# A two-layer decoder step on eight cores: channel-major residual, five blocks of 416 tokens, and one planned instruction order

## The chip, the cores and the metric

The kernel runs on all 8 cores of one Trainium2 chip. Each core takes one prompt sequence of 2048 tokens and four of the 32 sample sequences with 8 new tokens each, so 2080 tokens, and all the weights. The cores do not talk to each other. The metric is the device time of the slowest core, in microseconds (us).

Executions come in two states. In the fast state the eight cores lie within about 2% of each other. In the slow state the cores of one die (sometimes of both) show a lower granted TensorE clock and the time is some per cent longer.

## The reference, cut to what matters

```python
D_MODEL = 1024; SEQ = 2048; DEPTH = 2; D_FF = 4096; HEAD_DIM = 64
DIL_PAIRS = ((128, 1), (512, 4), (2048, 16))        # (window, dilation), 2 heads each
IN_COLS = 2560                                      # u 256 | q,k,v 3 x 384 | gates 3 x 384

def trunk_layer(x, pos, is_prompt, ...):
    h = rmsnorm(x, norm1_g)
    proj = h @ w_in                                 # split into u, q, k, v, gb, gc, gh
    y_pool = pool_mix(pool_hist, u, pos, ...)       # causal means over 2/4/8/16 rows
    q = partial_rope(rmsnorm(q, q_norm_g), pos)     # rotary on 16 of 64 dims
    k = partial_rope(rmsnorm(k, k_norm_g), pos)
    for g, (window, dil) in enumerate(DIL_PAIRS):   # keys at distance 0, dil, ..., window
        o, lse = dilated_attention(q[g], k[g], v[g], window, dil)
    y_attn = sum over g of softmax(lse)[g] * o[g]   # = sum of numerators / sum of denominators
    z = gc * gh; y_conv = gb * conv3(z)
    x = x + concat(y_pool, y_attn, y_conv) @ w_out  # 768 -> 1024
    hf = rmsnorm(x, norm2_g) @ w_up                 # 1024 -> 4096
    x = x + square(relu(hf)) @ w_down               # 4096 -> 1024
    # ... also returned: the shifted K/V caches, pool and conv states
```

## The kernel before

The kernel before works stage by stage. The residual X lies token-major (128 tokens by 1024 channels, 17 tiles, the last one 32 tokens). Every norm scales a tile and then turns it with TensorE transposes into HT, the channel-major operand of the next matmuls:

```python
for t in range(NTILE):                                  # norm_and_transpose, 17 tiles, 4 times a run
    S.op("dve", ... scalar_tensor_tensor(out=hb, in0=X[:, t, :], scalar=RSTD[:, t:t+1], in1=GBC, mult, mult))
    for c in range(8):
        S.op("pe", ... transpose(out=pst[:, c, 0:R], in_=hb[0:R, c*128:(c+1)*128], identity=IDB))
    S.op("act", ... copy(out=HT[:, :, 128*t:128*t+R], in_=pst[:, :, 0:R]))
```

Attention masks by adding a mask with a second matmul, and needs separate matmuls for the denominators:

```python
for (ki, kb) in kbs:                                    # att_unit, one of 16 per group
    matmul(pS[:, ki*256:+256], lhsT=K tile, rhs=Q of 2 heads, start=True, stop=False)
    matmul(pS[:, ki*256:+256], lhsT=IDB, rhs=MASKP, start=False, stop=True)       # mask
# ... exp ...
    matmul(pO[hs, 0:128], lhsT=VAUG[:, tk, h, 0:64], rhs=P, ...)                  # values
    matmul(pO[:, 128:256], lhsT=HSEL[:, h, :], rhs=P, ...)                        # denominators
# ... the three groups are summed into ACC by ACT or DVE, and divided after all of them
```

The MLP takes four blocks of 512 tokens and a last one of 32, for which the down projection still runs 512 columns wide:

```python
for fb in range(4):                 # 1024 hidden channels at a time
    up(0); copy_caches(l, fb)       # cache copies wait in hardware for the buffer ("at", 0)
    for b in range(5):              # b < 4: 512 tokens; b == 4: 32 tokens
        if b + 1 < 5: up(b + 1)     # 8 x 8 matmuls of blk_len(b) columns
        down(b)                     # per 128-token tile 2 x 8 matmuls of 512 columns, lhsT=at[:, fc, tile]
# ... the order of all instructions is the order in which this program text emits them
```

## Time and profile before

| | the kernel before |
|---|---|
| median of the first 3 runs | 1889.73 us (1887.67 to 1890.29) |
| TensorE (PE) busy | 1588.9 us, 84% of the span |
| VectorE (DVE) / ScalarE (ACT) busy | 47% / 32% |
| chain of work that ended last | PE 74%, DVE 8%, DMA 8% |

The page's busy times, then its strips of 40 slices (each digit the busy tenths of a slice; PEclk the granted TensorE clock in tenths; DMA the mean share of 16 engines), then the chain by engine:

```profile
PE 1588.9 (84%) x9076; PEld 806.7 (43%) x9076; DVE 895.9 (47%) x1593; ACT 599.9 (32%) x1255; POOL 199.0 (11%) x262
...
PE   0549768765899999999998985876579999999998
...
PEclk9979878957799999999997997895779999999999
DMA  9530001285440632603843000129544061260222
...
PE 74%; DVE 8%; DMA 8%; issue 5%; ACT 4%; POOL 1%; DVEq 0%; ACTq 0%; POOLq 0%; SPq 0%
```

The two runs of nines are the two MLPs. An average hides the rest, so here is the table of busy time by stretch. Each line has the stretch and its length in us, then per engine busy us and instructions, then the granted clock, the DMA share and GB/s:

```profile
core 6: us, PE busy (x) PEld busy (x) DVE busy (x) ACT busy (x) POOL busy (x), PEclk, DMA share, GB/s
0.00:88.00 88.00, 17.75 (x142) 13.56 (x143) 22.69 (x28) 38.16 (x58) 9.05 (x15) 1.00 0.77 165
395.00:446.00 51.00, 21.19 (x180) 12.38 (x178) 27.86 (x37) 12.10 (x29) 0.74 (x1) 0.50 0.66 161
494.00:520.00 26.00, 16.66 (x137) 12.83 (x138) 22.28 (x20) 17.42 (x20) 2.22 (x3) 0.56 0.80 122
520.00:990.00 470.00, 468.17 (x2368) 214.10 (x2366) 187.51 (x295) 101.30 (x194) 18.63 (x25) 0.99 0.40 72
1100.00:1342.00 242.00, 161.63 (x1255) 104.49 (x1255) 138.49 (x351) 125.22 (x321) 17.96 (x40) 0.77 0.31 79
1415.00:1887.00 472.00, 466.29 (x2368) 213.57 (x2366) 188.29 (x296) 83.43 (x162) 6.66 (x9) 1.00 0.30 63
```

So the MLPs (520 to 990 and 1415 to 1887) are TensorE at full clock with nothing to squeeze but the work itself. In the other 945 us TensorE is partly starved: in the end of attention (395 to 446) TensorE works 21 of 51 us at half clock, and in the norm stage (494 to 520) it works at a clock of 0.56. The trace shows the clock fall from 1.00 to 0.50 after a long pause and after short ones. At 496.9 us it falls in a pause of 4.7 us before the first transposes. At 377.4 us it falls too, and there no pause in the 15 us before lasted over 1.5 us; it stays at half through pauses of up to 2.9 us until 429 us. So a stream with many short pauses lost the clock here. The 1.00 of the first line isn't a measurement: the trace has no clock record before 90.7 us, and eight transposes took 1.01 us there, as they did from 498 us on at half clock.

In the chain inside an MLP, in order of time (start, duration, what), 64 matmuls of 512 columns (L1331, the down projection) take 13.81 us, 215.8 ns each. In the QKV stage, at full clock, 16 matmuls of 384 columns (L1014) take 2.61 us, 163.1 ns each. On the straight line through the two, 416 columns come to 176 ns, an estimate from these two numbers:

```profile
605.02 13.81 PE psum L1331 x64
```

```profile
338.74 2.61 PE psum L1014 x16
```

Two lines of the list of DMA issues (source, queue, count, KB each, median us to landing): the copies of the old caches (kv_s<-c, here the third of them that have 504 KB) and the pieces of w_out.

```profile
kv_s<-c SPq DMA_DIRECT2D x8, 504.0 KB, 9.4
...
big<-w_out POOLq DMA_DIRECT2D x6, 512.0 KB, 5.5
```

### The profile page before, as it was taken

To read this page: it belongs to the slowest core of one execution; us is meant where nothing else is said; L and a number is where in the kernel's file an instruction comes from. 1 tells how busy PE (TensorE), PEld (TensorE's weight loads), DVE (VectorE), ACT (ScalarE), POOL (GpSimd) and SP (SyncE) were. 2 spreads that over 40 slices of the span, in tenths; PEclk is the share of its full clock that TensorE was granted. 3 is DMA by queue.
4 is the path that set the end of the run, shared out by engine and by line. 5 is a ranking of instruction groups with operands and counts; after the bars stand their busy time and mean duration, and the time that the engine had idled before them with its cause. 6 is when DMAs were issued, how large, how long until landed. Compare 5 with 4: busy or idle time off the path is not lost.

```text
span 1887.7 us, 28589 instructions; the slowest of 8 cores (1875.0 to 1887.7 us)
## 1 busy us (share of the span) xinstructions
PE 1588.9 (84%) x9076; PEld 806.7 (43%) x9076; DVE 895.9 (47%) x1593; ACT 599.9 (32%) x1255; POOL 199.0 (11%) x262
## 2 busy tenths in 40 slices
PE   0549768765899999999998985876579999999998
PEld 0314445532444444444444443553244444444444
DVE  0427654736734444344337665473663443444433
ACT  3402356632521111212334235663252111121210
POOL 0147100000000000000003720000000000000000
PEclk9979878957799999999997997895779999999999
DMA  9530001285440632603843000129544061260222
GB/s 243 75 46 1 15 24 39 91 185 175 67 82 1 100 63 35 113 1 50 176 98 63 1 15 22 42 85 187 179 62 87 1 112 37 42 107 1 47 101 93
DMA packets 76348, 139.91 MB, mean 74 GB/s; under 512 B 28360, under 2 KB 41858, under 8 KB 75818
## 3 DMA queue, kind: packets, MB, share of 16 engines
q0 software_dynamic: 42144, 47.26, 17.5%
q1 hardware_dynamic: 34058, 90.83, 17.4%
q8 instruction: 77, 1.26, 0.3%
q14 instruction: 69, 0.57, 0.1%
HBM read 162.45 MB, written 44.75 MB: 110 GB/s over the span
## 4 chain that ended last, share of the span: by engine, by line
PE 74%; DVE 8%; DMA 8%; issue 5%; ACT 4%; POOL 1%; DVEq 0%; ACTq 0%; POOLq 0%; SPq 0%
PE psum L1331 25%; PE psum L1314 24%; PE psum L777 7%; PE psum L1014 7%; PE psum L1295 5%; DMA big<-w_in 5%; DVE big L714 2%; DMA big<-c 2%; DVE big L1270 1%; PE psum L720 1%; DVE big L1055 1%; ACT big L1023 1%; PE psum L1143 1%; DVE big L1157 1%; PE psum L1137 1%
## 5 line engine op out<-in xcount | busy, mean ns | idle before, releaser
L1331 PE MATMUL psum<-big 128*128 128x512 bf16 (+1 forms) x2176 | 477.4, 380 | 0.5 <-DVE big L1319 0.3
L1314 PE MATMUL psum<-big 128*128 128x512 bf16 (+1 forms) x2560 | 466.4, 340 | 1.5 <-DVE big L1319 1.3
L1318 ACT ACTIVATE big<-psum 128x512 f32<-128x512 f32 (+1 forms) x320 | 165.3, 517 | 690.0 <-PE psum L1314 681.6
L1319 DVE TENSOR_TENSOR big<-psum,big 128x512 bf16<-128x512 f32 (+1 forms) x320 | 189.2, 591 | 301.9 <-ACT big L1318 294.0
L1314 PEld LDWEIGHTS psum<-big 128*128 128x128 bf16 x2560 | 216.2, 98 | 249.6 <-issue 9.1
L1331 PEld LDWEIGHTS psum<-big 128*128 128x128 bf16 (+1 forms) x2176 | 211.9, 98 | 258.6 <-issue 6.3
L1333 DVE TENSOR_TENSOR big<-psum,big 128x512 f32<-128x512 f32 (+1 forms) x272 | 187.9, 691 | 261.4 <-PE psum L1331 261.2
L777 PE MATMUL psum<-big 128*128 128x512 bf16 (+1 forms) x880 | 166.0, 346 | 0.8 <-DVE big L897 0.4
L1014 PE MATMUL psum<-big 128*128 128x384 bf16 (+1 forms) x816 | 152.6, 347 | 15.2 <-ACT big L1023 6.7
L720 PE MATMUL psum<-big 128*128 128x128 bf16 (+1 forms) x544 | 66.0, 299 | 98.8 <-DVE big L714 98.0
L1014 PEld LDWEIGHTS psum<-big 128*128 128x128 bf16 (+1 forms) x816 | 96.0, 122 | 63.4 <-issue 31.8
L777 PEld LDWEIGHTS psum<-big 128*128 128x128 bf16 x880 | 75.2, 99 | 89.0 <-issue 9.4
L720 PEld LDWEIGHTS psum<-big 128*128 128x128 bf16 (+1 forms) x544 | 50.5, 136 | 115.4 <-issue 115.4
L1295 PE MATMUL psum<-big 128*128 128x512 bf16 (+1 forms) x408 | 93.7, 394 | 0.0
L714 DVE SCALAR_TENSOR_TENSOR big<-big 128x1024 bf16<-128x1024 f32 (+1 forms) x68 | 85.3, 1282 | 15.1 <-DMA big<-norm_g 9.4
L705 ACT ACTIVATE big<-big 128x1024 bf16<-128x1024 f32 (+1 forms) x51 | 53.9, 1057 | 76.2 <-DVE big L1297 58.3
L722 ACT COPY big<-psum 128x1024 bf16<-128x1024 bf16 (+1 forms) x68 | 65.9, 975 | 37.7 <-PE psum L720 37.7
L1157 DVE TENSOR_TENSOR big<-psum,big 128x256 f32<-128x256 f32 x64 | 39.2, 613 | 76.9 <-PE psum L1143 76.8
L667 POOL DMA_DIRECT2D big<-w_up x16 | 12.1, 758 | 586.6 <-PE psum L1314 329.3
L1297 DVE TENSOR_TENSOR big<-psum,big 128x512 f32<-128x512 f32 (+1 forms) x68 | 47.0, 691 | 48.9 <-PE psum L1295 48.9
L1295 PEld LDWEIGHTS psum<-big 128*128 128x128 bf16 (+1 forms) x408 | 40.8, 101 | 52.1 <-issue 7.7
L830 DVE SCALAR_TENSOR_TENSOR big<-big 64x512 bf16<-64x512 f32 (+1 forms) x40 | 35.7, 892 | 57.5 <-POOL big L817 50.5
(117 smaller groups left out, 1269.9 us busy)
## 6 DMA issues: line engine op xcount, KB each, us to landing
big<-xp SPq DMA_DIRECT2D x32, 512.0 KB, 12.2
big<-w_up POOLq DMA_DIRECT2D x16, 1024.0 KB, 11.0
big<-w_down POOLq DMA_DIRECT2D x16, 1024.0 KB, 15.6
kv_s<-c SPq DMA_DIRECT2D x8, 2040.0 KB, 20.1
big<-c SPq DMA_DIRECT2D x24, 512.0 KB, 5.2
xpark<-big SPq DMA_DIRECT2D x16, 512.0 KB, 3.7
big<-xpark SPq DMA_DIRECT2D x16, 512.0 KB, 9.7
yp<-big SPq DMA_DIRECT2D x16, 512.0 KB, 2.7
```

What stands on the lines that cost most here:

```text
L714: S.op("dve", lambda e, t=t, R=R, hb=hb: e.scalar_tensor_tensor(out=hb[0:R, :], in0=X[0:R, t, :], scalar=RSTD[0:R, t:t + 1], in1=GBC[0:R, ...
L720: S.op("pe", lambda e, c=c, R=R, hb=hb, pst=pst: e.transpose(out=pst[:, c, 0:R], in_=hb[0:R, c * 128:(c + 1) * 128], identity=IDB[0:R, 0:R ...
L722: S.op("act", lambda e, t=t, R=R, pst=pst: e.copy(out=HT[:, :, 128 * t:128 * t + R], in_=pst[:, :, 0:R]), reads=[("ps", pi)], writes=[("ht ...
L777: S.op("pe", lambda e, d=d, pi=pi, L=L: e.matmul(bank(pi)[:, 0:L], lhsT=WA[:, d, col0:col0 + 128], rhs=HT[:, d, blk_cols(b)], start=(d == ...
L1014: S.op("pe", lambda e, d=d, j=j, csel=csel: e.matmul(pqv[0:R, j, 0:384], lhsT=HT[:, d, csel], rhs=WQ[g][:, d, :], start=(d == 0), stop=(d ...
L1157: S.op("dve", lambda e: e.tensor_tensor(out=ACC[:, :, qsel], in0=pov, in1=ACC[:, :, qsel], op=ALU.add), reads=[("ps", po), "acc"], writes= ...
L1295: S.op("pe", lambda e, c=c, pi=pi, R=R, t=t, hf=hf: e.matmul(bank(pi)[0:R, :], lhsT=MIXT[:, c, tile_cols(t)], rhs=WO[:, c, 512 * hf:512 * ...
L1314: S.op("pe", lambda e, d=d, fc=fc, pi=pi, L=L: e.matmul(bank(pi)[:, 0:L], lhsT=WU[i][:, d, 128 * fc:128 * fc + 128], rhs=HT[:, d, blk_cols ...
L1318: S.op("act", lambda e, pi=pi, L=L, ri=ri: e.activation(out=RL[ri][:, 0:L], in_=bank(pi)[:, 0:L], func=AF.Relu), reads=[("ps", pi)], write ...
L1319: S.op("dve", lambda e, pi=pi, L=L, ri=ri, at=at, fc=fc: e.tensor_tensor(out=at[:, fc, 0:L], in0=bank(pi)[:, 0:L], in1=RL[ri][:, 0:L], op= ...
L1331: S.op("pe", lambda e, fc=fc, pi=pi, R=R, lo=lo, hf=hf, at=at: e.matmul(bank(pi)[0:R, :], lhsT=at[:, fc, lo:lo + R], rhs=WD[i][:, fc, 512 ...
L1333: S.op("dve", lambda e, pi=pi, R=R, t=t, hf=hf: e.tensor_tensor(out=X[0:R, t, 512 * hf:512 * hf + 512], in0=bank(pi)[0:R, :], in1=X[0:R, t ...
```

## The change

The intent: remove the transposes and the token tail, thin out the attention, and let a planner interleave stages that used to stand one after the other.

- **Channel-major residual.** X is kept as 8 x 128 channels by tokens, from input to output (the host lays the arrays out that way). The output and down projections now have the weights stationary and tokens as columns, so their results are channel-major too. The norm's sum over channels becomes a matmul with a matrix of ones in float32r; the 17 x 8 transposes of each norm go.
- **Five blocks of 416 tokens**: 5 x 416 = 2080, no tail.
- **Attention** on pairs of PSUM banks: the mask becomes a 0/1 multiplication on VectorE after the exponential; the value matmul's weights are [V | ones] (128 columns), so numerators and denominators of all three groups accumulate in two banks that stay held; one division per head and token block of 512.
- **Order from a plan.** Each stage is a generator with a priority. A simulation on the host with an assumed cost for each operation picks, at every moment, the ready operation of the lowest priority number for each engine. What comes out is a fixed order per engine; the semaphores between engines are real, so a wrong guess costs waiting. What the plan alone places, nothing holds.

The core of it as a diff, cut heavily (`...` marks cuts):

```diff
+LAT = {"pe": 0.25, "act": 0.12, "dve": 0.12, "pool": 0.15}
+class Planner:
+    def start(self, eng):                     # engine free, an operation ready
+        _, _, op, p = heapq.heappop(self.ready[eng])        # lowest priority number first
+        emit()                                # the instruction takes its place in the order
+        if len(op) > 3:                       # a DMA: 260 GB/s, one after the other, 2 us more
+            self.dma_free = max(self.dma_free, self.now) + nbytes / 260e3
+            done = max(self.dma_free, self.now) + 2.0
...
-        S.op("dve", ... scalar_tensor_tensor(out=hb, in0=X[0:R, t, :], scalar=RSTD, in1=GBC ...))
-        for c in range(8): S.op("pe", ... transpose(...))
-        S.op("act", ... copy(out=HT[:, :, 128 * t:128 * t + R], in_=pst))
+        for c in range(8):                    # norm(l, which, b): one block of 416 tokens
+            act(BL, activation(out=SQR[i], in_=X[:, b, c, :], func=Square))
+            pe(matmul(bank(bi)[:, 0:BL], lhsT=ONESR, rhs=SQR[i], start=(c == 0), stop=(c == 7)))   # float32r
+        act(Ln, scale=1/D, bias=EPS); act(Exp, scale=-0.5)
+        for c in range(8):
+            dve(scalar_tensor_tensor(out=HT[:, c, block b], in0=X[:, b, c, :], scalar=gain, in1=RST, mult, mult))
...
-    matmul(pS, lhsT=IDB, rhs=MASKP, start=False, stop=True)
-    matmul(pO[hs, 0:128], lhsT=VAUG[:, tk, h, 0:64], rhs=P)
-    matmul(pO[:, 128:256], lhsT=HSEL[:, h, :], rhs=P)
+    dve(tensor_tensor(out=P, in0=P, in1=MASKP, op=mult))
+    matmul(bank(6 + h)[...], lhsT=VREG[:, 8 * g + sl, 64 * h:64 * h + 128], rhs=P, start=first)   # [V | ones]
+    # att(): after all groups of a block of 512 tokens
+    RATT = exp(-ln(denominators))
+    dve(tensor_tensor(out=MIXT[hs, 2, c0:c0+512].rearrange("p (i r) -> p r i", r=16),
+                      in0=bank(6 + h)[hs] as (r i), in1=RATT[hs] as (r i), op=mult))
...
-    down: matmul(bank(pi)[0:R, :], lhsT=at[:, fc, lo:lo + R], rhs=WD[i][:, fc, 512 * hf:512 * hf + 512])
+    down: matmul(bank(bi)[:, 0:416], lhsT=WD[i][:, f, 128 * oc:128 * oc + 128], rhs=AT[a][:, f, :])
...
+    # mixer(l): priorities; lower comes first
+    K.spawn(norm(l, 0, b, ...), base + 2 + b)                 # base = 1000 * l
+    K.spawn(qkv(l, None, g, 0), base + 95)                    # the sample tokens' q, k, v
+    K.spawn(qkv(l, blk, g, pr), base + 100 + 50 * blk + 2 * g + pr)
+    K.spawn(seq(all of pool and conv done, load_wo(l, 2)), base + 400)     # the third piece of w_out
+    K.spawn(reload(l, b, done[b]), base + 300)                # x comes back for the residual
+    # mlp(l): the waits of the weight loads
+    if fb == 0: wu, wd = qk_done, att_done
...
-    copy_caches: S.dma(..., reads=[("at", 0)])                # waits in hardware
+    copy_caches: wait(ev("um", l, fb, 1, 0)) then ld(...)     # waits in the plan only
```

## The prediction

> **What bounds it now.** TensorE work, plus stages that starve it. The table of busy time by stretch (slowest core) splits 1887.7 us into two MLP stages of 470 and 472 us, where PE is busy 99% at a granted clock of 0.99 to 1.00, and about 945 us of everything else: 520 us before the first MLP, 425 us between the MLPs. In those 945 us PE is busy about 655 us, part of it slow: clock 0.52 to 0.60 in the norm-and-transpose stages (26, 27, 25 us), 0.50 in the ends of attention (50 us each, PE busy 21 to 23 us), and little before 88 us, where the chain is the serial w_in loads. Chain view: PE 74%.
>
> **MLP.** 64 matmuls of 512 columns take 13.81 us in the chain: 215.8 ns each. [...] Blocks of 416 should take 175.8 ns [...]. 5120 of them are 900 us, against 942 us: the change removes the tail (128 down matmuls of 512 columns for 32 tokens, and 512 small up matmuls). Gain about 40 us, all on the critical path.
>
> **Mixer, per layer, PE (estimates from the trace's rates).** Projections 440 x 175.8 ns = 77 us; QKV 408 x 163 ns = 66 (unchanged); output projection 240 x 175.8 = 42; attention about 35 to 40 (before 79: S, mask, value and denominator matmuls 158 us over two layers; mask matmuls go, value|ones merges two groups); sum-of-squares matmuls 80, 15 to 25 us (replacing 35 us of cold transposes); transposes, sample and pool 22. Sum about 265 us. DVE about 225 to 240 us (a 512-column op 0.69 us, scaled), ACT 185, POOL 80: PE stays the limit, DVE close behind. In before the attention stretch (1100 to 1342 us) kept PE busy for only 160 of 242 us, as stages were separate. The plan interleaves them; I expect 80 to 85% PE density: 310 to 330 us per mixer instead of 425.
>
> **Edges.** Start: x (8.5 MB) and weights at the 237 GB/s seen in the first 40 us; the WQ pieces still wait for each other (5.1 us each alone). QKV comes first, so PE works from about 35 us and the projections from about 110 us; I charge 50 us. Layer change: norms of blocks 0 to 3 run under the last MLP blocks; 10 to 15 us left of 27. Tail 8 us.
>
> **Sum.** 50 + 315 + 450 + 12 + 315 + 450 + 8 = 1600 us; I say 1595. Range 1530 to 1670 (8 in 10). Faster by over 2%: 0.95; within 2%: 0.03; slower: 0.02.
>
> **What would show it.** MLP: two stretches of about 450 us, PE 99%, 176 ns a matmul, clock 1.0. Mixers: PE busy 80 to 85%, clock above 0.9, no stretch at 0.5. PE busy in total about 1430 us. Output projection running into the MLP without a gap. ACT and DVE each below 75% in the mixers.
>
> **What would make it wrong.** [...] (b) The order is fixed from assumed costs; where a DVE, POOL or DMA step is later than planned, PE waits in order and falls to half clock: 30 to 60 us a mixer. (c) DVE with POOL beside it slows (a 512-column op with three operands took 0.87 to 1.05 us against 0.69), making DVE the limit. (d) Start loads slower than charged. (e) Better than thought: density of 90% gives 1540.

## The result, and the profile after

| | before | after |
|---|---|---|
| fast runs | 1887.67 to 1890.29 us (4 runs) | 1700.05, 1700.66, 1706.17 us |
| slow runs | none of the four | 1933.25, 1925.86, 1816.41 us |
| PE busy, slowest core | 1588.9 us (84%) | 1458.2 us (86%) |
| DVE / ACT / POOL busy | 47% / 32% / 11% | 52% / 28% / 15% |

The ratio of the fast runs is 0.901, with a 95% interval of 0.899 to 0.904. Ratios here are the mean time of one kernel's fast runs over that of the other's of the same rounds, so not quite the ratio of the medians quoted. The kernel became 10% faster, but its 1700 us lie 105 us above the predicted 1595 and above the range.

```profile
PE 1458.2 (86%) x8668; PEld 811.5 (48%) x8668; DVE 874.8 (52%) x1637; ACT 482.4 (28%) x1065; POOL 247.3 (15%) x342
...
PE   4466679629999999999997677876999999999998
...
PEclk9777999969999999999997889998999999999999
DMA  8662310599923206015154341007999320500022
...
PE 68%; DVE 11%; DMA 8%; issue 6%; POOL 4%; ACT 3%; DVEq 0%; ACTq 0%; SPq 0%; POOLq 0%
```

The nines of the MLPs are shorter, and the wide valleys at half clock are gone but for one slice just before the first MLP (the 2 among the PE digits, clock 6, DMA 9). Below it is the stretch from 349 to 383:

```profile
core 5: us, PE busy (x) PEld busy (x) DVE busy (x) ACT busy (x) POOL busy (x), PEclk, DMA share, GB/s
0.00:135.00 135.00, 64.61 (x247) 32.56 (x247) 50.99 (x122) 45.99 (x118) 39.62 (x63) 0.81 0.75 137
135.00:349.00 214.00, 161.97 (x1243) 95.18 (x1244) 149.05 (x295) 86.87 (x204) 74.99 (x98) 0.93 0.26 58
349.00:383.00 34.00, 2.49 (x10) 0.74 (x8) 5.17 (x3) 1.50 (x3) 1.46 (x2) 0.57 1.02 212
383.00:431.00 48.00, 47.70 (x255) 25.87 (x256) 29.36 (x52) 13.86 (x26) 0.00 (x0) 0.95 1.03 169
431.00:885.00 454.00, 454.00 (x2581) 252.53 (x2580) 202.48 (x348) 95.13 (x187) 22.27 (x28) 1.00 0.33 60
886.00:925.00 39.00, 30.42 (x101) 14.80 (x101) 21.24 (x34) 24.84 (x51) 10.43 (x20) 0.74 0.56 110
925.00:1182.00 257.00, 192.39 (x1362) 109.77 (x1360) 179.49 (x384) 104.23 (x266) 89.16 (x120) 0.89 0.28 53
1182.00:1238.00 56.00, 49.29 (x293) 27.02 (x293) 34.29 (x55) 15.56 (x29) 0.00 (x0) 0.90 1.02 226
1238.00:1692.00 454.00, 454.00 (x2581) 252.48 (x2579) 201.86 (x347) 94.33 (x184) 8.90 (x12) 1.00 0.31 63
```

(The 0.81 of the first line is too high, for the first 50 us have no clock record and count as 1.00: eight QKV matmuls took 2.74 us at 47.6 us, as they did at 61.4 us at half clock, 2.72 us; at 77 us, at full clock, sixteen took 2.97 us.)

Read it as two copies of the same work. From 0 to 431 us TensorE is busy for 277 us, from 886 to 1238 for 272 us (sums of the lines). The work is nearly the same; the waiting differs. In layer 0, TensorE is idle for 70 us up to 135, 52 us from 135 to 349 and 32 us from 349 to 383: 154 us in all. In layer 1 it is idle for 9, 65 and 7 us: 80 us. The first layer loses 74 us more, at its start and at its end.

From the time lines, the savings against the kernel before are: the stretch before the first MLP 520 to 431, the first MLP 470 to 454, between the MLPs 425 to 353, and the second MLP with the tail 472 to 460. That is 89 + 16 + 72 + 12 = 189 us.

In the chain, 128 matmuls of the MLP (L1318, the up projection) take 22.51 us, 175.8 ns each. At the MLP's start something stands between every 8 of them:

```profile
660.57 22.51 PE psum L1318 x128
```

```profile
431.61 1.42 PE psum L1318 x8
433.22 1.42 PE psum L1318 x8
```

Groups of 1.42 us start 1.61 us apart. In the 0.19 us between them stands one float32r matmul of 416 columns (a sum of squares of a later block), which the timeline shows there. So a float32r matmul costs about as much as a bf16 one (175.8 ns). Its weight load took 190 ns there on average (bf16: 98 ns), overlapped.

The chain of the start (start, duration, what), then the one step at the end of the first mixer:

```profile
4.89 11.98 DMA big<-w_in
...
17.41 21.32 DMA big<-w_in
...
68.41 5.44 DMA big<-w_in
...
73.98 2.72 PE psum L971 x8
```

```profile
349.44 33.72 DMA big<-w_out
```

What TensorE waited for (line, releaser, total us, times, longest), and the landings:

```profile
PE psum L799 <- ACT sqr L796: 38.7, 34, 9.7
PE psum L1302 <- DMA big<-w_out: 25.5, 1, 25.5
PE psum L971 <- DMA big<-w_in: 19.9, 2, 10.7
...
PE psum L1152 <- DVE big L1216: 8.8, 4, 3.6
...
PE psum L1302 <- DVE big L1216: 6.4, 1, 6.4
```

```profile
kv_s<-c SPq DMA_DIRECT2D x8, 504.0 KB, 56.9
...
big<-w_out POOLq DMA_DIRECT2D x6, 512.0 KB, 10.2
```

L971 is the QKV matmul, L1302 the output projection, L1216 the last division of attention, L1152 the value matmul, and L799 and L796 the sums of squares and the squares. The cache copies of 504 KB now take 56.9 us to land instead of 9.4, and all 24 copies are issued from 356.5 us on (for layer 0) and 1187.8 us on (for layer 1): before the MLP, not in it. Of the six w_out pieces the worst, the last one of layer 0, lands after 33.7 us. The last one of layer 1 lands after 10.1 us: there is no such stall before the second MLP.

### The profile page after: what moved, and what is told of

It reads as the page before. It is cut to its first block, busy times and chain, and to the rows that moved or that the text cites. A ratio compares the mean times of both kernels' runs of the same rounds, so it can differ in the third digit from the quotient of the medians.

```text
span 1697.8 us, 27200 instructions; the slowest of 8 cores (1680.6 to 1697.8 us)
## 1 busy us (share of the span) xinstructions
PE 1458.2 (86%) x8668; PEld 811.5 (48%) x8668; DVE 874.8 (52%) x1637; ACT 482.4 (28%) x1065; POOL 247.3 (15%) x342
## 4 chain that ended last, share of the span: by engine, by line
PE 68%; DVE 11%; DMA 8%; issue 6%; POOL 4%; ACT 3%; DVEq 0%; ACTq 0%; SPq 0%; POOLq 0%
PE psum L1318 27%; PE psum L1334 27%; PE psum L1302 5%; DMA big<-w_in 4%; PE psum L841 4%; PE psum L971 3%; DVE big L1019 2%; DMA big<-w_out 2%; POOL big L1011 2%; PE psum L799 2%; DVE big L1216 1%; DMA big<-spool 1%; DVE big L1005 1%; DMA big<-vspill 1%; DVE big L995 1%
## 5 line engine op out<-in xcount | busy, mean ns | idle before, releaser
L1318 PE MATMUL psum<-big 128*128 128x416 bf16 x2560 | 463.5, 339 | 0.0
L1334 PE MATMUL psum<-big 128*128 128x416 bf16 x2560 | 460.7, 339 | 0.0
L1323 ACT ACTIVATE big<-psum 128x416 f32<-128x416 f32 x320 | 165.4, 517 | 667.8 <-PE psum L1318 435.6
L1334 PEld LDWEIGHTS psum<-big 128*128 128x128 bf16 x2560 | 249.5, 98 | 199.9 <-issue 2.1
L1318 PEld LDWEIGHTS psum<-big 128*128 128x128 bf16 x2560 | 248.2, 98 | 200.1 <-issue 4.8
L1324 DVE TENSOR_TENSOR big<-psum,big 128x416 bf16<-128x416 f32 x320 | 188.2, 591 | 296.2 <-ACT big L1323 286.2
L1337 DVE TENSOR_TENSOR big<-psum,big 128x416 f32<-128x416 f32 x320 | 188.5, 591 | 204.4 <-PE psum L1334 203.9
L971 PE MATMUL psum<-big 128*128 128x384 bf16 (+1 forms) x816 | 167.8, 368 | 37.8 <-DMA big<-w_in 19.9
L841 PE MATMUL psum<-big 128*128 128x416 bf16 x880 | 182.3, 360 | 12.8 <-DVE big L1005 3.5
L971 PEld LDWEIGHTS psum<-big 128*128 128x128 bf16 (+1 forms) x816 | 85.8, 108 | 108.3 <-issue 70.7
L1302 PE MATMUL psum<-big 128*128 128x416 bf16 x480 | 97.0, 353 | 38.2 <-DMA big<-w_out 25.5
L841 PEld LDWEIGHTS psum<-big 128*128 128x128 bf16 x880 | 87.5, 103 | 84.5 <-issue 31.6
L796 ACT ACTIVATE sqr<-big 128x416 fp32r<-128x416 f32 x160 | 84.7, 544 | 144.5 <-PE psum L799 86.7
L818 DVE SCALAR_TENSOR_TENSOR big<-big 128x416 bf16<-128x416 f32 x160 | 95.2, 668 | 53.7 <-ACT big L817 52.7
L799 PE MATMUL psum<-sqr,onesr 128*128 128x416 f32 x160 | 84.4, 556 | 39.1 <-ACT sqr L796 38.7
L1011 POOL TENSOR_TENSOR big<-big 128x512 f32<-128x512 f32 (+1 forms) x54 | 67.8, 1257 | 141.2 <-DVE big L1005 121.5
L1302 PEld LDWEIGHTS psum<-big 128*128 128x128 bf16 x480 | 44.7, 100 | 80.6 <-issue 51.9
L1304 DVE TENSOR_TENSOR big<-psum,big 128x416 f32<-128x416 f32 x80 | 45.2, 590 | 63.6 <-PE psum L1302 60.6
L799 PEld LDWEIGHTS psum<-sqr,onesr 128*128 128x128 f32 x160 | 36.1, 226 | 67.5 <-issue 60.7
```

Source lines behind the costliest of these rows:

```text
L799: return pe([(BL, lambda e: e.matmul(bank(bi)[:, 0:BL], lhsT=ONESR[:, :], rhs=SQR[:, i * BL:(i + 1) * BL], start=(c == 0), stop=(c == 7)), ...
L818: yield ops(*[dve(BL, lambda e, c=c: e.scalar_tensor_tensor(out=HT[:, c, BL * b:BL * b + BL], in0=X[:, b, c, :], scalar=NG[:, l, which, c: ...
L841: yield ops(pe([(BL, lambda e, d=d: e.matmul(bank(bi)[:, 0:BL], lhsT=WA[:, d, col0:col0 + 128], rhs=HT[:, d, BL * b:BL * b + BL], start=(d ...
L971: yield ops(pe([(384, lambda e, d=d, j=j, jj=jj: e.matmul(pq[0:R, jj, 0:384], lhsT=lhs(d, j), rhs=WQ[g][:, d, :], start=(d == 0), stop=(d ...
L1011: yield ops(pool(256 * J, lambda e: e.tensor_tensor(out=qf[0:R, 0:J, 0:256], in0=qf[0:R, 0:J, 0:256], in1=GQK[0:R].unsqueeze(1).to_broadca ...
L1302: yield ops(pe([(BL, lambda e, c=c: e.matmul(bank(bi)[:, 0:BL], lhsT=WO[c // 2][:, c % 2, 128 * oc:128 * oc + 128], rhs=MIXT[:, c, BL * b: ...
```

## The experiments

All are variations of the changed kernel, each run on the same chip. "Ratio" is against the kernel before, from fast runs; the changed kernel itself stands at 0.901. Times are means of fast runs. All outputs agreed with the reference but for one experiment. Every edit is planned anew. In the traces of div_order and copy_pinned the instructions of every engine still stand in the order of the changed kernel; in the others the order can move as well, so a control (plan_shift) comes with them.

The time of the slowest core jitters: in some fast runs one or two cores run an MLP at a clock of 0.97 or 0.98 and end 10 to 20 us late. The mean over the fast runs of the median core is steadier, so the overview gives both (us). The starts of the MLPs are those of the slowest core of the profiled run.

| | slowest core | median core | first MLP starts | second MLP starts |
|---|---|---|---|---|
| the changed kernel | 1702 | 1690 | 431 | 1238 |
| norm_early | 1710 | 1695 | 428 | 1241 |
| div_order | 1687 | 1676 | 425 | 1227 |
| wo_first | 1701 | 1693 | 419 | 1238 |
| smp_late | 1679 | 1666 | 401 | 1218 |
| copy_pinned | 1691 | 1682 | 423 | 1227 |
| tail_order | 1678 | 1670 | 409 | 1213 |
| w_burst | 1701 | 1694 | 401 | 1239 |
| plan_shift | 1703 | 1689 | 417 | 1229 |
| three_fixes | 1652 | 1643 | 388 | 1187 |
| four_fixes | 1652 | 1638 | 392 | 1185 |
| burst_fixes | 1666 | 1658 | 412 | 1210 |
| rope_one | 1633 | 1624 | 385 | 1175 |
| start_order | 1674 | 1665 | 404 | 1213 |
| wq_burst3 | 1676 | 1667 | 407 | 1216 |
| slow_w20 | 1650 | 1643 | 391 | 1185 |
| slow_w15 | 1648 | 1642 | 384 | 1186 |

### 1. norm_early: the second layer's norms before the last MLP blocks

The prediction wanted the norms of layer 1 to run under the last MLP blocks; their priority (1002 and up) puts them behind all of the MLP.

```diff
-K.spawn(norm(l, 0, b, src, ev("ht", l, b), before), base + 2 + b)
+K.spawn(norm(l, 0, b, src, ev("ht", l, b), before), base + 2 + b if l == 0 else base - 500 + b)
```

> One number of the plan changed: the norms that open layer 1 get precedence over the MLP of layer 0 in the plan. In the changed kernel the sum-of-squares matmuls of all five blocks stand behind the last MLP matmul in TensorE's order (they start at 885 us), so the first QKV matmul of layer 1 starts at 924 us. Theory A (the layer change costs about 40 us instead of the predicted 12 because of this order): the norms of blocks 0 to 3 run under the MLP, QKV of layer 1 starts within about 20 us of the end of the MLP, and the kernel gets 15 to 30 us faster (1670 to 1685 us). Rival (the mixer's length is set by its own work and memory, so a sooner start only makes it wait elsewhere): under 8 us.

Measured: 1710 us, ratio 0.905 [0.903, 0.908] (four fast runs; one slow run of 1810). The layer change itself did shrink as meant: the first QKV of layer 1 starts 8 us after the MLP's end instead of 39 (the first MLP takes 460 us instead of 454 for it). But the second MLP starts at 1241 us instead of 1238. The chain at the end of the mixer holds stores and the reload of x:

```profile
1157.16 11.00 DMA pool_p<-big
1169.29 16.49 DMA conv_p<-big
1187.70 29.16 DMA big<-xpark
```

What follows: the 30 us of the layer change were not a loss that adds to the total, as the rival expected: from its first QKV to the second MLP the mixer took 344 us instead of 314. That the DMA work at its end is the reason is not shown here; four_fixes tests it.

### 2. div_order: the last division writes contiguously

L1216 writes its bf16 result in steps of 16 elements (32 bytes). The edit moves the steps to the float32 inputs.

```diff
-dst = MIXT[hs, 2, c0:c0 + 512].rearrange("p (i r) -> p r i", r=16)
+dst = MIXT[hs, 2, c0:c0 + 512].rearrange("p (i r) -> p i r", r=16)
-    out=dst, in0=bank(6 + h)[hs].rearrange("p (r i) -> p r i", r=16), in1=RATT[hs].rearrange("p (r i) -> p r i", r=16), op=ALU.mult),
+    out=dst, in0=bank(6 + h)[hs].rearrange("p (r i) -> p i r", r=16), in1=RATT[hs].rearrange("p (r i) -> p i r", r=16), op=ALU.mult),
```

> Only the order in which the last division of attention walks its elements is changed (16 instructions, same operands; the output is now written contiguously, and PSUM and the reciprocal are read with a stride; before, the output was written with a stride of 32 bytes). In the changed kernel one takes 2305 ns, where 512 columns elsewhere take 689 ns. Theory: the strided 2-byte write is what is slow, so it falls to 0.7 to 0.8 us, 25 us of VectorE time goes away, and 5 to 15 us of the total, since attention blocks take turns on one pair of accumulators. Rival: strided reads cost the same, or it is something else in the instruction: stays near 2.3 us and the time does not move.

Measured: 1687 us, ratio 0.893 [0.891, 0.895] (four fast runs), 15 us less than the changed kernel's 1702 (mean of its three fast runs). The group's line (busy us, mean ns) in the changed kernel, and in this one:

```profile
L1216 DVE TENSOR_TENSOR big<-psum,big 64x512 bf16<-64x512 f32 x16 | 36.9, 2305 | 7.9 <-ACT big L1210 7.0
```

```profile
L1216 DVE TENSOR_TENSOR big<-psum,big 64x512 bf16<-64x512 f32 x16 | 16.2, 1016 | 7.5 <-ACT big L1210 6.6
```

What follows: the same elements cost 2305 ns with the strided write and 1016 ns with the contiguous one. 20.7 us of VectorE work go, and 15 us of time. The division releases the two held banks, and some three quarters of its gain was on the way. The expected 0.7 to 0.8 us a division did not come; what the strided reads cost in the 1016 ns, no run here says.

### 3. wo_first: x reloads only after the last piece of w_out

```diff
-K.spawn(reload(l, b, done[b]), base + 300)
+K.spawn(reload(l, b, done[b] + [ev("wo", l, 2)]), base + 300)
```

> The reload of the residual x waits in the plan for the last piece of w_out. In the changed kernel that piece is asked for at 349 us of layer 0 behind reloads and MLP weights, lands 33.7 us later, and TensorE waits 25.5 us for it (34 us with only 2.5 us of PE work). Theory B (queued behind other transfers): it lands in about 10 us, the output projection starts 20 us sooner, 10 to 25 us of gain if x is then not late. Rival (the DMA engines are full there, 170 to 212 GB/s, so whichever comes last ends the wait): the wait moves to the reload of x, gain under 8 us.

Measured: 1701 us, ratio 0.901 [0.899, 0.902] (three fast runs, one slow of 1801). The last piece of w_out lands within 16.5 us, and the wait moves on to the additions that need x:

```profile
PE psum L1302 <- DVE big L1304: 30.8, 2, 16.3
```

The first MLP starts 12 us sooner, the second at the same 1238 us (the control below moves the first as far for no reason).

What follows: putting one of two equally urgent transfers first gained nothing in all. What has to move is something that is not urgent.

### 4. smp_late: the sample tokens' QKV behind the first prompt ones (layer 0)

TensorE keeps the order that it is given: in the trace of the changed kernel its 8668 matmuls stand in one and the same order on all eight cores, though these take from 1680.6 to 1697.8 us. The three sample QKV groups stand first and need the QKV weights of all three groups, of which the last piece lands at 74 us. TensorE stood for them for 10.7 and 9.2 us, and the QKV of the first prompt block came behind them, at 77 us.

```diff
-K.spawn(qkv(l, None, g, 0), base + 95)
+K.spawn(qkv(l, None, g, 0), base + 107 if l == 0 else base + 95)
```

> In layer 0 the QKV of the 32 sample tokens comes after that of the first prompt block in the plan (before: ahead of it, so that TensorE, which works in order, stands at 50 us until the weights of group 1 land at 61 us and of group 2 at 74 us, though block 0 and the weights of group 0 are there). Theory C (order): the first QKV of block 0 starts at about 50 us instead of 77, and the kernel gets 8 to 20 us faster. Rival (start is limited by the arrival of weights and by GpSimd standing at its own DMA waits): TensorE starts earlier but stalls a few us later, gain under 6 us.

Measured: 1679 us, ratio 0.888 [0.883, 0.893] (four fast runs from 1668 to 1692): 24 us less. The first MLP starts at 401 us instead of 431. TensorE's wait for w_in is now:

```profile
PE psum L971 <- DMA big<-w_in: 12.3, 2, 8.5
```

What follows: the order at the start is worth 24 us. The wait for w_in on TensorE itself fell by only 7.6 us (19.9 to 12.3), so most of the gain lies elsewhere. By stretches of the two traces, TensorE idles 7 us less from 48 to 80 us, 4 less from 80 to 135, 11 less from there to the mixer's end (at 340 us before, at 315 now) and 5 less in that end. Why the middle gained most, the run doesn't say.

### 5. copy_pinned: the cache copies held in hardware

The plan meant the copies for the MLP, yet nothing in hardware holds them there, and they are issued at 356.5 us. The edit gives them back a real wait, on a buffer that the MLP writes, as the kernel before had.

```diff
+def pinned(fn, key, slot):
+    S.dma(fn, reads=[key], slot=slot)
+    S.regions[key].readers.pop(("dma", slot), None)
-yield ops(ld(lambda e: e.dma_start(out=o_kv_s[g][l, n, 0:W - 8, :], in_=caches[g][l, n, 8:W, :]), 2000 * W, slot=("c2c", g)))
+yield ops(("sp", 0.06, lambda: pinned(lambda e: e.dma_start(...), ("at", fb * NB % 2, 7), ("c2c", g)), 2000 * W))
```

> The copies of the caches from input to output (24 transfers, 21 MB read and written in all) get a real wait: each reads a piece of the MLP's activations as a pretext, as in the kernel before. In the changed kernel the plan places them beside the MLP, but no wait holds them there, so the queue issues all 12 of a layer at 356 to 369 us and 1188 to 1200 us, in the middle of the reload of x and the load of the last w_out piece and the first MLP weights; they land in 62 us (median) against 9 in the kernel before, and DMA is full from 349 to 431 us. The order of every other engine is the same. Theory D (the copies starve the end of each mixer): the last w_out piece lands in under 20 us instead of 33.7, the MLP of layer 0 starts 10 to 25 us sooner, that of layer 1 0 to 10 sooner; total 10 to 30 us faster. Rival (w_out stands behind 4 MB of w_down and x alone, which are there anyway): under 5 us.

Measured: 1691 us, ratio 0.897 [0.894, 0.899] (three fast runs, one slow of 1773): 11 us less. The order of the computing engines is unchanged, so this is the one experiment with nothing moved but the copies. They are issued from 437 us on (but the first three of layer 1 at 1176 us, before its MLP at 1227: their wait had been met already), the 504 KB ones land in a median of 8.0 us, the slowest piece of w_out lands after 26.9 us instead of 33.7, and the w_out wait shrinks from 25.5 us:

```profile
PE psum L1302 <- DMA big<-w_out: 19.0, 1, 19.0
```

What follows: the copies did crowd the end of the first mixer, but they were the smaller part of its stall.

### 6. tail_order: the copies held, and the first w_down behind the last w_out

The last piece of w_out waits until pooling and convolution are done, and the first w_down pieces stand in the same queue.

```diff
 # on top of copy_pinned
-wu, wd = qk_done, att_done
+wu, wd = qk_done, att_done + [ev("wo", l, 2)]
```

> As copy_pinned, and the first w_down is asked for only after the last piece of w_out in the plan. If w_out's lateness in layer 0 comes from its place behind w_down in the same queue, the wait of 25.5 us goes away here and the MLP of layer 0 starts at 405 to 412 us instead of 431; if the copies alone did it, this adds under 4 us to copy_pinned. If the x reload is the next in line, the wait moves to it and both are small.

Measured: 1678 us, ratio 0.891 [0.888, 0.893] (four fast runs): 24 us less, 13 of them beyond copy_pinned. The first MLP starts at 409 us instead of 431, as expected. (In this plan five of the 24 copies, at 353 and 1161 us, still slip out before their MLP.)

```profile
PE psum L1302 <- DMA big<-w_out: 7.2, 1, 7.2
```

What follows: the stall of 349 to 383 us was for the most part a queue order, an urgent 1 MB (w_out is float32 in memory) behind and beside transfers that are needed only later. The pieces of w_out land within 15.7 us instead of 33.7.

### 7. w_burst: all pieces of one weight issued together

The pieces of one QKV weight wait for each other although they write different columns. The edit issues them together.

```diff
-for j in range(3): yield ops(ldc(... piece j ..., w=[("wq", g)], slot=("wq", g)))
+yield ops(("pool", 2.4, lambda: S.dmas([three pieces], writes=[("wq", g)], slot=("wq", g), queue="pool"), 3 * 524288))
 # and the same for the two pieces of each WA quarter
```

> The three pieces of each QKV weight and the two of each quarter of the projection weight are issued together, with no wait of GpSimd for the landing of the piece before. In the changed kernel those waits stand in GpSimd's queue (71 and 36 us in all) ahead of its part of the QKV work, and the last QKV piece lands at 74 us. Theory E (serial loads): the last QKV piece lands by about 55 us, the projections start by 95 us instead of 116, and the total falls 10 to 25 us. Rival (in the first 40 us DMA moves 242 GB/s already, x among it, so bandwidth sets the arrival): the QKV weights come at about the same time, x later, gain under 6 us. The plan's order shifts as well, so the stage times count more than the total.

Measured: 1701 us, ratio 0.902 [0.899, 0.905] (two fast runs; three slow ones of 1750 to 1883). The first MLP starts at 401 us, 31 us sooner (TensorE begins with projections at 65 us, QKV at 87). From there to the second MLP it takes 31 us longer, for a reason that we know from layer 0:

```profile
1151.47 39.64 DMA big<-w_out
```

What follows: a gain in the first layer was handed back at the end of the second mixer. Without the profile by stages this would read as "no effect". With only two fast runs the total is the least certain of this list.

### 8. plan_shift: the control

```diff
-LAT = {"pe": 0.25, "act": 0.12, "dve": 0.12, "pool": 0.15}
+LAT = {"pe": 0.35, "act": 0.12, "dve": 0.12, "pool": 0.15}
```

> A control: the plan assumes 0.35 us instead of 0.25 for the end of a TensorE step to be seen, nothing else. Every engine's order shifts (hundreds of lines) for no reason that any theory names. It shows how far a shuffled order alone moves the time: I expect within 8 us of the changed kernel's 1700. If it moves by 20 us or more, gains of 10 to 15 us in the runs that change the plan can't be put down to their one reason.

Measured: 1703 us, ratio 0.903 [0.900, 0.906] (four fast runs), though the two MLPs start at 417 and 1229 us instead of 431 and 1238. In its profile the slowest core then ran the second MLP at a clock of 0.98 and took 471 us for it; the median core stands at 1689 us, against 1690.

What follows: a mere reshuffle left the total where it was, while stage ends moved by 9 to 14 us on the profiled core. One control is little, but it says to trust totals and the median core more than single stage ends.

### 9. three_fixes: smp_late, div_order and tail_order together

> smp_late, div_order and tail_order together. Alone they took 24, 14 and 22 us off 1701. If each removes a wait of its own, the sum gives 1640 us (1632 to 1650): the MLP of layer 0 starts at about 375 us, that of layer 1 about 325 to 335 after the end of the first. If they remove the same wait twice, it stays above 1660.

Measured: 1652 us, ratio 0.875 [0.872, 0.877] (four fast runs from 1647 to 1656, one slow of 1837): 50 us less than the changed kernel, against 63 as the sum of the three alone (24 + 15 + 24), and just outside the expected 1632 to 1650. By the median core it is 47 against 58. The first MLP starts at 388 us, the second at 1187 us.

```profile
48.00:110.00 62.00, 32.99 (x142) 15.93 (x139) 22.49 (x63) 13.22 (x43) 20.44 (x30) 0.70 0.59 76
...
327.00:388.00 61.00, 49.40 (x263) 26.46 (x263) 33.46 (x58) 15.51 (x29) 1.55 (x3) 0.89 0.72 167
```

What follows: they mostly add. The hole before the first MLP is mostly closed: 49 of the last 61 us are work now, where it was 50 of 82 (the lines 349 to 431 of the changed kernel). The start, 33 of 62 us at a clock of 0.70, is still starved.

### 10. four_fixes: norm_early on top of the three

> three_fixes plus norm_early, which alone gained nothing: QKV of layer 1 began 27 us sooner after the MLP (9 instead of 39 us) and all of it was lost again at the end of that mixer (the output projection took 65 us instead of 55, with DMA full and the reload of x landing after 29 us). Theory D says the crowded end swallowed it: with the end freed, 10 to 25 us below three_fixes. Rival (the mixer's middle, about 73% PE busy, is set by chains through the other engines that do not start sooner): within 6 us of three_fixes.

Measured: three fast runs at 1646 to 1657 us and one of 1671 us; the latter is 1.5% above the fastest and so counts as slow, but the ratio 0.879 [0.874, 0.884] is of rounds that hold it too. The mean of the three is that of three_fixes, and the median core gains 5 us. The first QKV of layer 1 now starts 8 us after the MLP, and the stretch between the MLPs is 333 us instead of 345. But the first MLP takes 460 us instead of 454, because 48 sums of squares instead of 19 now run inside a stage that is all TensorE, and it starts 4 us later. The mixer from its first QKV to the second MLP takes 325 us instead of 306.

What follows: in an MLP with TensorE busy 100% there is no room under it. The 29 moved matmuls cost 6 us there, their full time of 0.2 us each. That is little beside the 32 us by which QKV starts sooner after the MLP; 19 of these are lost in the mixer, although its end was freed. So theory D's gain did not come, and the total is the rival's. What makes that mixer longer, no run here shows.

### 11. burst_fixes: div_order, tail_order, norm_early and w_burst

> w_burst with div_order, tail_order and norm_early (not smp_late). Alone w_burst brought the MLP of layer 0 forward by 31 us (401 instead of 431) and lost 31 in layer 1, where the last w_out piece took 39.6 us to land. With w_out ahead of w_down and the copies held back, that loss should go: 1630 to 1650 us, and w_out's wait in layer 1 under 10 us. If the loss was a shuffled order and not w_out, it stays above 1665.

Measured: 1666 us, ratio 0.882 [0.879, 0.885] (three fast runs, one slow of 1722). The expectation was missed. The first MLP starts at 412 us. In the new plan TensorE begins with projections at 66 us and comes to QKV at 87 us only (three_fixes: QKV at 48).

What follows: on this order, issuing the weights together was no substitute for smp_late.

### 12. rope_one: one rotary product of four

Three of the four rotary multiplications are left out, on top of three_fixes. The outputs are wrong (relative error 0.54); the question is what VectorE's time is worth.

```diff
-... for k, a, b in ((0, x1, cs), (1, x2, sn), (2, x2, cs), (3, x1, sn))])
+... for k, a, b in ((0, x1, cs),)])
```

> three_fixes with one of the four rotary multiplies left (wrong result on purpose): 162 VectorE instructions of 0.29 us less, 23 us a mixer. In the changed kernel VectorE is busy 60 to 75% in the mixers. If VectorE is the limit there (risk c of the prediction), both mixers shorten by about 15 to 23 us each, 30 to 45 in all. If the mixers wait on chains of small steps and on DMA, it is 0 to 12 us, about one step less of 1 us per QKV pair where a chain ends late.

Measured: 1633 us, ratio 0.865 [0.862, 0.867] (four fast runs): 19 us less for 44 us of VectorE work removed (busy 811 us instead of 855).

What follows: this lies between the two theories. VectorE isn't the limit of the mixers throughout, or all 44 us would have come off. Its chains do hold TensorE back for some of the time.

### 13 and 14. start_order and wq_burst3: more of the start by order of loads

Both are three_fixes with the pieces of each QKV weight issued together; start_order also makes x blocks 2 to 4 wait for the weights.

```diff
 # start_order only
+    reads=[("wq", b - 2)] if b >= 2 else [],     # on the loads of x
 # both
+yield ops(("pool", 2.4, lambda: S.dmas([three pieces], writes=[("wq", g)], ...)))
```

> On three_fixes: the pieces of a QKV weight are issued together, and blocks 2 to 4 of x wait (in hardware too) for the QKV weights of groups 0 to 2. Before the first QKV matmul then 3.4 MB of x and 1.6 MB of weights move instead of 8.5 MB and 1.6 MB. Theory F (the start is set by what shares the DMA engines ahead of the first QKV weight; 240 GB/s in the first 40 us): the first QKV matmul comes at 28 to 36 us instead of 47, the last QKV weight by 55 us instead of 72, and the MLP of layer 0 starts 8 to 18 us before three_fixes' 388. Rival (the norms and the chains through GpSimd, VectorE and ScalarE set the first 130 us): first QKV sooner, but the MLP starts within 5 us of 388.

> On three_fixes: only the pieces of a QKV weight issued together, x as before. Theory F: with x's 8.5 MB still in front, the first QKV matmul comes at 42 to 50 us as before; the last QKV weight lands somewhat sooner (60 to 68 us instead of 72); MLP of layer 0 within 8 us of 388. If it comes near start_order, the serial waits were the cause and not the share of bandwidth.

Measured: 1674 us (ratio 0.886 [0.884, 0.889], four fast runs) and 1676 us (0.888 [0.884, 0.891], three fast, one slow of 1783). Both are 22 to 24 us slower than three_fixes, and both expectations were missed. The plan now puts projections in front: they begin at 61 and 65 us, QKV at 95 and 99 us instead of 48. TensorE then stood at projections whose weights were late, for 33.5 us (start_order) and 44.3 us (wq_burst3), where three_fixes waited 15.5 us for w_in.

What follows: neither order of loads was a gain. As the edits turned over TensorE's order too, the runs don't price the load order by itself; they show once more what TensorE, held to the plan's order, pays for a weight that the plan took to be there.

### 15 and 16. slow_w20 and slow_w15: tell the plan that these loads are slow

The plan charges a piece of w_in, 512 KB in memory, 4.0 us (its constants: 2.0 us at 260 GB/s and 2.0 us more). In the trace of the changed kernel the first layer's pieces in the chain took 4.6 to 21.3 us. The edit, on top of three_fixes, doubles the bytes that the plan assumes for the w_in pieces of layer 0, or takes 1.5 times.

```diff
-... in_=wv[:, :, c0:c0 + 128]), 524288, w=[("wq", g)], ...
+... in_=wv[:, :, c0:c0 + 128]), int(524288 * (1 if l else 2)), w=[("wq", g)], ...      # slow_w15: 1.5
 # the same for the two pieces of WA
```

> On three_fixes: the plan alone is told that the QKV and projection weights of layer 0 have twice their bytes (1 MB instead of 0.5 for a QKV piece), so that it expects them later; the transfers are the same. The plan assumes 260 GB/s and 2 us to landing; in the first 75 us the chip lands a 0.5 MB piece in 5 to 21 us. Theory G (an order made for weights that come too soon sets TensorE in front of late weights): TensorE's waits for w_in before 200 us fall from 15.5 us to under 8, the MLP of layer 0 starts 5 to 15 us before three_fixes' 388, total 1637 to 1650. In start_order and wq_burst3 the same theory explains their loss of 21 to 24 us: there the plan expected weights sooner still, and TensorE waited 33 to 44 us for projection weights. Rival (start is bandwidth and chains whatever the order): within 5 us of 388.

> As slow_w20 with 1.5 times the bytes. Theory G: between three_fixes and slow_w20 in the waits for w_in; if its total lies on the other side of three_fixes from slow_w20's, the order's accidents are as large as the effect.

Measured: 1650 us (0.872 [0.866, 0.878], four fast runs) and 1648 us (0.870 [0.866, 0.875], three fast, two slow of about 1750), against 1652 us. The wait on w_in is halved, to 8.0 us in slow_w20 and 6.8 us in slow_w15 (first line three_fixes, then slow_w15):

```profile
PE psum L971 <- DMA big<-w_in: 15.5, 2, 9.7
PE psum L971 <- DMA big<-w_in: 6.8, 1, 6.8
```

What follows: with that wait down from 15.5 to 6.8 us the total moves by no more than the noise, and slow_w20's first MLP starts at 391 us, not 5 to 15 us before 388. Theory G's part about the waits came out about as expected, its gain did not. Three_fixes and slow_w15 can't be told apart, and both beat both kernels: 50 to 54 us under the changed one, 13% under the kernel before.

Some further variants (other DMA rates in the plan, QKV sooner, no rotary at all) never ran. Either the plan ran into a deadlock, or a memory check before the run found a read of data not yet written. The latter would mean that some orderings rest on the plan's assumed times alone, as those of the cache copies do, so a new plan has to be verified, not only timed.

## Why the prediction was right or wrong

**Right: the MLP.** 175.8 ns a matmul, as predicted; 454 us a stage against 450. The 4 us more are the sums of squares at its start. TensorE at 100%, clock 1.00 (0.99 to 1.00 on all eight cores of this fast run from 460 to 880 us).

**Right in number, partly by luck: a mixer by itself.** From the first QKV of layer 1 at 924 us to the second MLP at 1238 us it is 314 us; the prediction said 315. But the prediction counted the first norm in it, which stands before that point. From the end of the first MLP the mixer holds 272 us of TensorE work, close to the predicted 265, and takes 353 us, where 12 + 315 = 327 us were charged.

**Missed: density.** 272 of 353 us are 77%, as are 242 of the 313 us from 925 to 1238 us; 80 to 85% was expected. The clock was 0.89 from 925 to 1182 us, not above 0.9. VectorE stayed below 75%, as expected (179 of those 257 us).

**Refuted: risk (a), that the float32r matmuls are slow or their weight loads not hidden.** The matmuls ran at about the bf16 rate, 0.19 us each inside the MLP (bf16: 175.8 ns), with their weight loads of 190 ns overlapped.

**Wrong: "Start: ... I charge 50 us".** This is the term that failed. The events that it named came 13 and 6 us late (QKV from 48 us instead of 35, projections from 116 instead of 110), but the sum went on as if the full mixer rate held from 50 us. The first MLP starts at 431 us; less a mixer of 314 us, the start cost 117 us, 67 more than charged. (The other terms: layer change 27 us more, the two MLPs 8 more, mixer and tail 3 less; together 99 above the sum of 1600.) By the table of stretches, 70 us of idle TensorE lie before 135 us, and 25 us more than in layer 1 lie at the mixer's end, in a stall that wasn't in the sum at all.

What the runs showed in its place: three things, each measured alone and then together. The order at the start put the sample QKV, which needs the last weights, first (24 us). The end of the first mixer had its last w_out piece behind w_down and beside copies that nothing held (24 us over both layers, 11 of them the copies). The last division wrote in strides at 2305 ns instead of 1016 (15 us). Together they are 50 us of the 105, and 43 of these lie before the first MLP (388 us instead of 431). The rest of the miss stays open.

**Wrong in size: "norms of blocks 0 to 3 run under the last MLP blocks; 10 to 15 us left".** They stood behind the MLP in the plan, and the layer change took 39 us. norm_early and four_fixes show what this is worth alone: nothing in the total, as the mixer after it gets longer by 30 and 19 us. And a TensorE that is 100% busy has no "under": there the 29 moved matmuls cost their full time, 6 us.

**Right as a warning: risks (b) and (d).** The order is fixed from assumed costs, and loads came later than assumed. The prediction named both and put neither into its sum. Risk (c), VectorE as the limit, was half right: rope_one gave back 19 of 44 us. The slowing itself stands in the trace of the kernel before, for one operation and not for another: the 128x512 operation of VectorE at L891 took 736 to 744 ns in the five cases where GpSimd was idle, and 908 ns on average (736 to 1561) in the 36 where GpSimd was busy for over half of it, while the one at L883 took 691 ns in both cases.

**Open.** Some 50 us between the best version, 1648 us, and the predicted 1595. The start has no cheap order left that these runs found: the first 48 us move 213 GB/s, and until 110 us TensorE is half idle. What share of that is bandwidth, what share VectorE's chains, no run here separates. Why smp_late gained 24 us when its own wait fell by 8, and why the mixer of layer 1 gets longer when it starts sooner, isn't settled either.

## What to carry to other kernels

Cost the first pass through a repeated stage by itself: sum the work and the idle time by stretch, and set it against the second pass: the difference is what the first one alone pays. When a planner orders instructions, look at each transfer that only the plan holds back, and at what stands in the same queue in front of an urgent one. A stage with TensorE at 100% is no place to hide TensorE work (29 matmuls moved into one cost 6 us here), and a gain in one stage has to be followed to the end of the run before it counts.
